# First and second score block of a head pair at one place, the third two steps behind, in a hybrid decoder layer

## The chip, the cores and the metric

The kernel runs on one core of one Trainium2 chip. The metric is the device time of one execution in microseconds; a version's time is the median of its runs. In the profile's rows PE is TensorE's matmuls, PEld its weight loads, DVE is VectorE, ACT is ScalarE, POOL is GpSimd, SP is SyncE, whose queue starts most DMAs.

## The reference

One decoder layer over a sequence of 1024 positions and 1024 channels, in float32. A normalised input goes through one large projection into eight groups of 1024 channels; two token mixers run beside each other and are merged by gates; an output projection and a squared-ReLU MLP follow. The change lies in the second mixer, a gated linear recurrence over 8 heads of 128 channels:

```python
def hybrid_mixer(h, lower_bound, w_in, ...):
    proj = h @ w_in
    xa, ga, q, f, v, g, m_a, m_b = jnp.split(proj, SPLIT_POINTS, axis=-1)
    y_a = rg_lru(causal_depthwise_conv(xa, conv_w, conv_b), ...) * gelu(ga)
    f_gate = lb + (1.0 - lb) * sigmoid(f)
    o = rms_norm(hgrn2_chunkwise(silu(q), (1.0 - lb) * sigmoid(-f), log(f_gate), v), hg_norm)
    y = sigmoid(m_a) * y_a + sigmoid(m_b) * (o * silu(g))
    return y @ w_out

# hgrn2_chunkwise, one chunk; cum is the cumulative sum of log f inside the chunk
o_inter = einsum('bhtk,bhkv->bhtv', qc * exp(cum), state)
decay = where(causal, exp(min(cum_t - cum_s, 0)), 0)
scores = einsum('bhtsk,bhsk->bhts', qc * decay, kc)
o_intra = einsum('bhts,bhsv->bhtv', scores, vc)
state = exp(last) * state + einsum('bhsk,bhsv->bhkv', kc * exp(min(last - cum, 0)), vc)
```

## The kernel before

The sequence is cut into two halves `c` of 512 positions and the heads into four pairs `p`, which makes eight head pairs `i = 4 * c + p`, 0 to 7. Matrix products in full precision are made of three matmuls each (`mm3`, lines 148 to 150: high by high, high by low, low by high parts), mostly with 128 weights' columns and 512 moving columns: the wide matmuls of the rows.

`stage(i)` is a generator that gives TensorE the projections of pair `i`: the values `v` of the pair before (16 steps, from the second pair on), then `xa` (8 steps), `q` (8 steps), five steps of `f`, the gates of the first mixer (`rg_lru`) and the rest of `f`. A step of a projection is two `mm3`, six wide matmuls. Other engines' work hangs between: ScalarE's copies of the convolution's input (`conv_in`), VectorE's convolution (`conv`, line 573), weight loads on SP's queue with their split into high and low parts (`fill_w`, line 92), and GpSimd's sums (`make_combos`). After the last pair, `last_stage` takes the place of a further stage; its first steps are `v` and the gate projection `g`.

`hgrn(c, p, got, go)` is the second mixer for one pair. It prepares decayed copies of queries and keys on VectorE (`q1`, `qa`, `qb` and `kk`, `kb`, `kc`, mostly by `mul`, line 668) and computes the scores inside groups of 2, 8 and 32 positions by three blocks of small matmuls (`blocks`, line 678): `pt1` from `kk` and `q1`, `pt2` from `kb` and `qa`, `pt8` from `kc` and `qb`. A block is 32 matmuls with 32 weights' columns and 48 moving columns, which the profile shows as 64 records; its results lie in one PSUM bank, for `pt1` and `pt2` one of the two with the tag `sc`. `own_block` (lines 668 and 689, tile `dd`) copies `pt1` under a mask on VectorE, `level_blocks` (line 697) does so for `pt2` and `pt8`. After `pt8` has read `kc` and `qb`, these are multiplied on in place, then `kk` and `qf` are made for the coarser blocks of lines 798 and 809; then come the transposes of `kk` (835), the state's products (845, added up on VectorE in lines 854 and 856) and the outputs (870, 873).

The interleaving is written out by hand: `go(n)` runs `n` steps of the next pair's stage, so the stage's matmuls fill the time between `hgrn`'s own. `GO`, `GO_FIRST` (pair 0) and `GO_SECOND_HALF` (pairs 4 to 7) hold the step counts; their first number is the step behind which `pt8` stands (26, in pair 0 it is 16, since stage 1 has no `v`), the second the steps from `pt8` to line 798. In the version before, `pt1` stands four steps and `pt2` two steps ahead of `pt8`.

TensorE's order in this part is the written one (`pin` keeps it in program order). The order on the other engines is set when the program is built, by a planner that takes the instruction of the smallest priority (the place in the program, or 400 places earlier under `tc.high_priority(400)`) among those that its own estimate of times finds ready. Engines run their queues in order and wait on semaphores.

## Time and profile before

| | |
|---|---|
| median of 3 runs | 1538.94 us (1538.2 to 1539.3) |
| the profiled execution: its time, its span | 1538.52 us, 1536.7 us |
| TensorE, busy share of the span | 99% |
| VectorE, ScalarE, GpSimd | 75%, 52%, 10% |
| granted TensorE clock | 0.998 |
| the first and the last score block of `pt1` begin at | 81.2 and 507.5 us |

A row of the timeline has the start, the duration, the engine, the line, the operation, the tile written and those read, the shapes and a count; in brackets stands the idle time of the engine ahead of it and what ended it. Matmuls overlap in their pipeline: a wide one is shown with 0.39 us, but the next one begins 0.23 us after it. A row of waits has the waiting engine with its tile and line, the one waited for, the sum in us, how often, and the longest. Rows of a line or a tile give the count and the least, median and largest duration in ns, and the first and last start.

### The profile page before, as it was taken

The numbers are of one execution on the slowest core, as the hardware profiler recorded it, in microseconds if no ns is written. First come the engines' busy times: TensorE is split into PE (matmuls) and PEld (weight loads), VectorE is DVE, ScalarE is ACT, GpSimd is POOL, SyncE is SP. The second block draws the span as 40 slices with busy tenths as digits, with TensorE's granted clock in tenths as the row PEclk, the third lists the DMA queues.
The fourth block names the chain that finished last, engine by engine and source line by source line (L and its number), as shares of the span: only waits on it lengthen the run. The fifth ranks groups of instructions, "written<-read, shape, count | busy, mean of one in ns | idle before, by whom it ended". The sixth has DMA issues, their size and how long they took to land. (4 is left out here: it accounts for less than half of the span.)

```text
span 1536.7 us, 23202 instructions
## 1 busy us (share of the span) xinstructions
PE 1522.4 (99%) x9085; PEld 1275.2 (83%) x9085; DVE 1149.0 (75%) x1656; ACT 804.6 (52%) x1341; POOL 153.6 (10%) x188
## 2 busy tenths in 40 slices
PE   9999999999999999999999999999999999999997
PEld 7878988889889888888888888888888788888886
DVE  6798695485675838786856578888888898888877
ACT  6646757567567335454533447666666721111115
POOL 1022210232624600000000000000000000000000
PEclk9999999999999999999999999999999999999999
DMA  8545455465674274432338324666666685666642
GB/s 298 200 153 193 150 193 200 147 217 174 224 232 140 99 298 165 151 137 83 137 106 329 127 110 161 261 251 249 249 253 247 229 308 223 249 252 251 250 182 110
DMA packets 81679, 306.82 MB, mean 200 GB/s; under 512 B 8481, under 2 KB 20897, under 8 KB 68642
## 3 DMA queue, kind: packets, MB, share of 16 engines
q1 hardware_dynamic: 77536, 292.75, 52.0%
q10 hardware_dynamic: 4034, 12.59, 2.1%
q8 instruction: 71, 1.16, 0.3%
q14 instruction: 38, 0.31, 0.1%
HBM read 201.50 MB, written 103.81 MB: 199 GB/s over the span
## 5 line engine op out<-in xcount | busy, mean ns | idle before, releaser
L1680 DVE TENSOR_TENSOR acc<-acc,dX 128x512 f32<-128x512 f32 x128 | 85.3, 686 | 28.2 <-PE dX L150 27.8
L87 ACT CAST wA<-q 128x512 fp32r<-128x512 f32 x46 | 28.5, 620 | 136.1 <-PE dX L150 101.6
L92 DVE TENSOR_TENSOR wL<-raw,wH 128x1024 fp32r<-128x1024 f32 x46 | 56.3, 1226 | 40.7 <-ACT wH L87 39.8
L87 ACT CAST wH<-raw 128x1024 fp32r<-128x1024 f32 x46 | 48.2, 1049 | 33.8 <-DMA raw<-wts_in 14.9
L1680 DVE TENSOR_TENSOR acc<-acc,dY 128x512 f32<-128x512 f32 x64 | 43.5, 687 | 13.3 <-PE dY L150 13.1
L148 PE MATMUL po<-wH,y 128*128 128x512 f32 x128 | 49.9, 393 | 0.0
L149 PE MATMUL po<-wL,y 128*128 128x512 f32 x128 | 49.9, 389 | 0.0
L150 PE MATMUL po<-wH,y 128*128 128x512 f32 x128 | 49.7, 390 | 0.0
L1531 ACT ACTIVATE b<-b 128x512 f32<-128x512 f32 x48 | 30.0, 625 | 29.2 <-DVE b L1530 29.0
L92 DVE TENSOR_TENSOR wA<-q,wA 128x512 fp32r<-128x512 f32 x46 | 31.5, 687 | 15.2 <-ACT wA L87 15.1
L112 ACT CAST wH<-raw 128x1024 fp32r<-128x1024 f32 x36 | 37.7, 1047 | 8.3 <-issue 3.7
L179 POOL TENSOR_TENSOR rstd_h<-rstd_h,mhalf 128x1 f32<-128x1 f32 x8 | 4.6, 583 | 370.8 <-DVE rstd_h L174 370.8
L573 DVE SCALAR_TENSOR_TENSOR xc<-xp,pvt,xc 128x512 f32<-128x512 f32 x48 | 40.2, 849 | 1.1 <-ACT xc L557 1.1
L1089 DVE TENSOR_TENSOR s<-q,q 128x512 f32<-128x512 f32 x46 | 31.7, 688 | 4.4 <-DMA q<-mlp_in 4.0
L486 POOL TENSOR_TENSOR stt<-r,stt 128x256 fp32r<-128x256 f32 x16 | 19.8, 1260 | 126.4 <-ACT stt L485 114.2
L1097 DVE TENSOR_TENSOR s<-q 128x512 f32<-128x512 f32 x46 | 31.6, 687 | 0.2
L1532 ACT ACTIVATE b<-b 128x512 f32<-128x512 f32 x48 | 30.1, 630 | 1.0
L877 ACT ACTIVATE on<-po 128x128 f32<-128x128 f32 x64 | 16.8, 277 | 26.1 <-PE po L873 26.0
L150 PEld LDWEIGHTS po<-wH,y 128*128 128x128 f32 x128 | 24.0, 188 | 5.0
L149 PEld LDWEIGHTS po<-wL,y 128*128 128x128 f32 x128 | 24.1, 188 | 4.8
L148 PEld LDWEIGHTS po<-wH,y 128*128 128x128 f32 x128 | 24.0, 188 | 4.8
L1179 DVE TENSOR_TENSOR gb<-gY,ge 128x512 f32<-128x512 f32 x14 | 9.7, 691 | 23.7 <-PE gY L150 23.7
(2562 smaller groups left out, 5439.1 us busy)
## 6 DMA issues: line engine op xcount, KB each, us to landing
q<-mlp_in SPq DMA_DIRECT2D x92, 512.0 KB, 3.7
raw<-wts_in SPq DMA_DIRECT2D x80, 512.0 KB, 5.0
rest<-wL SPq DMA_DIRECT2D x36, 512.0 KB, 2.9
wL<-rest SPq DMA_DIRECT2D x36, 512.0 KB, 4.3
hd<-ri SPq DMA_DIRECT2D x16, 256.0 KB, 3.5
od<-onT ACTq DMA_DIRECT2D x8, 512.0 KB, 6.6
cdT<-stT SPq DMA_DIRECT2D x16, 256.0 KB, 3.2
o<-od SPq DMA_DIRECT2D x4, 1024.0 KB, 7.2
```

The costliest lines, as they stand in the source:

```text
L87: ins = A.copy(h, src)
L92: ins = V.tensor_tensor(out=lo, in0=src, in1=h.bitcast(F32), op=ALU.subtract)
L112: A.copy(h, raw)
L148: pin(PE.matmul(o, ah, bh, start=first, stop=False, **how))
L149: pin(PE.matmul(o, ah, bl, start=False, stop=False, **how))
L150: pin(PE.matmul(o, al, bh, start=False, stop=last, **how))
L573: ins = V.scalar_tensor_tensor(xc[:, s, :], xp[:, j : j + T], pvt[:, PV_CW + 8 * j + u : PV_CW + 8 * j + u + 1], xc[:, s, :], op0=ALU.mult ...
L1089: ins = V.tensor_tensor(out=sa[:, 0, :], in0=a21, in1=a22, op=ALU.add)
L1097: V.tensor_tensor(out=sb[:, 0, :], in0=a21, in1=a11, op=ALU.add)
L1531: A.activation(b[:, at, :], b[:, at, :], AF.Relu, scale=-1.0 if at == 2 else 1.0)
L1532: A.activation(b[:, at, :], b[:, at, :], AF.Square)
L1680: V.tensor_tensor(out=dst, in0=dst, in1=banks[bk, pr], op=op)
```

## The change

`pt1` moves two steps back, directly ahead of `pt2`, so that both blocks stand together two steps ahead of `pt8`. Two pairs have places of their own: in pair 0 both stand three steps ahead of `pt8` (`pt1` one step later than before, `pt2` one earlier), in pair 6 both stand four steps ahead (`pt1` where it was, `pt2` two steps earlier). `pt8` and all that follows keep their steps. No instruction is added or removed.

```diff
+SCORES_AT = {0: (1, 0, 3), 6: (0, 0, 4)}
...
         at = GO_FIRST if first else GO_SECOND_HALF if c else GO
-        between = 2
-        go(at[0] - 2 * between)
+        before_1, before_2, before_8 = SCORES_AT.get(4 * c + p, (2, 0, 2))
+        go(at[0] - 4 + before_1)
         pt1 = blocks(kk, lambda k: q1[:, 16 * k : 16 * k + 16, :], "1")
-        go(between)
+        go(before_2)
         pt2 = blocks(kb, lambda k: qa[:, k * g0 // 32 : (k + 1) * g0 // 32, 1:7, :], str(c0))
-        go(between)
+        go(before_8)
         pt8 = blocks(kc, lambda k: q4[:, k * g1 // 32 : (k + 1) * g1 // 32, 1:7, :], str(c1), "hg")
...
-        go(at[1])
+        go(at[1] + 4 - before_1 - before_2 - before_8)
```

## The prediction

> **What bounds the kernel now.** I read the head of the page first, then TensorE's own waits in the stretch of the eight head pairs (70 to 540 us), then the order of its instructions around the score blocks.

> ```profile
> span 1536.7 us, 23202 instructions
> ...
> PE 1522.4 (99%) x9085; PEld 1275.2 (83%) x9085; DVE 1149.0 (75%) x1656; ACT 804.6 (52%) x1341; POOL 153.6 (10%) x188
> ```
> ```profile
> PE po L870 <- DVE sn L856: 0.9, 1, 0.9
> PE sc L809 <- DVE qf L668: 0.5, 1, 0.5
> PE pkv L845 <- ACT kT L840: 0.2, 1, 0.2
> ```

> The reader is to see that TensorE is the bound, and that in 470 us of mixer work only three waits of it are recorded, one of each kind. All three fall in pair 0 (their rows stand below, at 97.86, 104.39 and 110.15 us). Outside pair 0, then, anything that shortens TensorE's own stream shortens the kernel by the same amount, until some other engine comes too late. So the change is priced in TensorE's stream, and then I look for what becomes late. Pairs are numbered 0 to 7; A, B and C are the first, second and third score block (`sc<-q,kk`, `sc<-qa,kb` and `sc<-qb,kc` in the rows).

> **The price of one block.** These are rows of TensorE's timeline in pair 1 (start, duration, engine, line, operands, count), and the row of all A blocks in the answer for line 678:

> ```profile
> 137.70 0.39 PE L150 MATMUL pj_xa<-hT01H,wL 128*128 128x512 f32 x1
> 138.02 0.89 PE L678 MATMUL sc<-q,kk 128*32 128x48 f32 x64
> 138.84 0.50 PE L148 MATMUL pj_xa<-hT01H,wH 128*128 128x512 f32 x1
> 139.18 0.40 PE L149 MATMUL pj_xa<-hT01L,wH 128*128 128x512 f32 x1
> ...
> 139.64 0.40 PE L148 MATMUL pj_xa<-hT01H,wH 128*128 128x512 f32 x1
> 139.87 0.39 PE L149 MATMUL pj_xa<-hT01L,wH 128*128 128x512 f32 x1
> ...
> 141.46 0.39 PE L150 MATMUL pj_xa<-hT01H,wL 128*128 128x512 f32 x1
> 141.78 0.89 PE L678 MATMUL sc<-qa,kb 128*32 128x48 f32 x64
> ```
> ```profile
> L678 PE MATMUL sc<-q,kk x512: 205/206/231, 81.2 to 508.2; 128*32 128x48 f32 x171
> ```

> Twelve wide matmuls (two steps) lie between A and B. Their steady spacing is (141.46 - 139.64)/8 = 0.2275 us. From the wide matmul ahead of A (137.70) to the fifth one behind it (139.87) are 2.17 us; five wide spacings are 1.137 us; so A costs 1.035 us. The records of A themselves take less: the first starts at 138.02, the last at 138.02 + 0.89 - 0.21 (the median duration) = 138.70, that is 0.68 us for 64 records or 10.8 ns each. The remaining 0.355 us is the price of going from wide to narrow matmuls and back: 0.32 in place of 0.23 us ahead of the block, 0.14 us from its last record to the next wide one, and 0.34 in place of 0.23 us after that.

> **What the joining saves.** With B directly behind A, one way back and one way in are gone. If B's records go on at A's pace, B costs 0.68 in place of 1.035 us, and a pair saves 0.355 us. No row shows two blocks of this shape in a row. One bound is that inner pace; the other is the nearest joint of two narrow blocks, line 798 followed by line 809:

> ```profile
> 153.38 0.70 PE L798 MATMUL sc<-qb,kc 128*32 128x32 f32 x32
> 154.01 1.15 PE L809 MATMUL sc<-qf,kk 128*64 128x64 f32 x16
> ```

> Its last record starts about 0.20 us ahead of its end, at 153.88, so the joint took 0.13 us where one record inside A takes 0.011. By that, a pair saves 0.235 us. These two have different shapes (weights of 32 and of 64 columns), A and B have the same, so I take 0.355, the row that is nearest. [...]

> Pair 2 differs, because A stands behind transposes there:

> ```profile
> 134.32 1.03 PE L186 MATMUL xT_x<-ident,xn 128*128 128x128 f32 x8
> 135.11 0.48 PE L148 MATMUL pj_xa<-hT01H,wH 128*128 128x512 f32 x1
> ...
> 200.22 1.03 PE L186 MATMUL xT_x<-ident,xn 128*128 128x128 f32 x8
> 201.19 0.89 PE L678 MATMUL sc<-q,kk 128*32 128x48 f32 x64
> 202.00 0.50 PE L148 MATMUL pj_xa<-hT01H,wH 128*128 128x512 f32 x1
> ```

> From the transposes to the next wide matmul are 0.79 us without A and 1.78 us with it, so A costs 0.99 us plus the 0.02 us by which the second spacing differs: 1.01. Moved to B, the two cost 1.715 in place of 1.01 + 1.035, and pair 2 saves 0.33 us.

> **What the move makes late.** A's products are read on VectorE by the masked copy `dd<-sc,mf` (lines 668 and 689). Where A ends later, VectorE stops there, with everything queued behind: the copies of B and C (line 697), the convolution (573), and the products `kc`, `qb`, `kk`, `qf` that lines 798 and 809 wait for. The tightest of these are pairs 4 and 5, where the products take 1.23 us each. Rows of pair 4 on VectorE and TensorE, and VectorE's wait for score blocks in pairs 3 to 6:

> ```profile
> 325.94 0.42 DVE L668 TENSOR_TENSOR dd<-sc,mf 128x256 f32<-128x256 f32 x1
> ...
> 328.68 0.45 DVE L697 COPY_PREDICATED dd<-mu,sc 128x192 f32<-128x192 uint8 x1 [1.84 <-PE sc L678]
> ...
> 339.66 1.23 DVE L668 TENSOR_TENSOR qf<-qb,seg 128x512 f32<-128x512 f32 x1
> ```
> ```profile
> 327.72 0.89 PE L678 MATMUL sc<-qa,kb 128*32 128x48 f32 x64
> ...
> 342.67 1.15 PE L809 MATMUL sc<-qf,kk 128*64 128x64 f32 x16
> ```
> ```profile
> DVE dd L697 <- PE sc L678: 7.3, 4, 1.8
> ```

> Today VectorE copies A at once and then sits idle 1.84 us for B. Changed, A begins at 327.72 - 1.035 = 326.69 and is done 0.89 us later, at 327.58. VectorE then waits about 1.65 us ahead of A's copy, spends 0.9 us on it and comes to B at about 328.5, where B has been ready since 328.26. That is 0.2 us ahead of today's 328.68: one wait takes the place of the other. `qf` ends at 340.89 - 0.2, line 809 wants it at 342.67 - 0.355, and 1.6 us of slack are left. Pairs 3 and 5 go the same way. In pair 6 A keeps its place and B comes two steps earlier, so VectorE's idle time shrinks and nothing is late. The three others:

> ```profile
> 142.77 1.23 DVE L92 TENSOR_TENSOR wL<-raw,wH 128x1024 fp32r<-128x1024 f32 x1 [1.70 <-ACT wH L87]
> ...
> 206.39 0.43 DVE L668 TENSOR_TENSOR dd<-sc,mf 128x256 f32<-128x256 f32 x1
> ...
> 514.15 0.41 DVE L668 TENSOR_TENSOR dd<-sc,mf 128x256 f32<-128x256 f32 x1
> ```

> In pair 1 A is done at 141.78 - 1.035 + 0.89 = 141.64, and its copy fits into the 1.70 us in which VectorE waits for ScalarE until 142.77 anyway. In pairs 2 and 7 A's copy runs at 206.39 and 514.15, while the later A would be done at about 201.19 + 2.73 + 0.89 = 204.8 and 508.2 + 2.73 + 0.2 = 511.1 (2.73 us are the two steps): covered. What A is moved past otherwise: ScalarE's four copies of the convolution's input, in pair 7 one part of GpSimd's combinations, in pair 0 a weight load on SP's queue with its split; none of them waits for A. C keeps its step and comes 0.355 us earlier. I price all of this at nothing.

> **Pair 0.** Here TensorE already waits for others. Rows of TensorE, of VectorE, and the busy time of each engine in a window (PE, PEld, DVE, ACT, POOL):

> ```profile
> 96.21 0.39 PE L150 MATMUL pj_f<-hT01H,wL 128*128 128x512 f32 x1
> 96.65 0.70 PE L798 MATMUL sc<-qb,kc 128*32 128x32 f32 x32
> 97.86 1.12 PE L809 MATMUL sc<-qf,kk 128*64 128x64 f32 x16 [0.51 <-DVE qf L668]
> ...
> 104.39 2.05 PE L845 MATMUL pkv<-v,kT 128*128 128x128 f32 x16 [0.20 <-ACT kT L840]
> ...
> 110.15 0.57 PE L870 MATMUL po<-v,scT 128*128 128x128 f32 x3 [0.94 <-DVE sn L856]
> ```
> ```profile
> 97.01 0.70 DVE L668 TENSOR_TENSOR qf<-qb,seg 128x512 f32<-128x512 f32 x1
> ```
> ```profile
> 65.50:102.70 37.20, 36.64 (x389) 29.80 (x388) 37.08 (x67) 21.28 (x33) 5.51 (x6) 1.00 0.51 181
> ```

> VectorE is busy for 37.08 of 37.20 us: it does not wait for TensorE here, so a TensorE that is 0.355 us early at line 798 waits 0.355 us more, and the three waits behind it are set by the same queue. Pair 0 saves nothing as long as the order of VectorE's work stays. That order is the planner's, and the edit can shift it. Bounds: if all waits went, pair 0 would give 0.355 us and the waits themselves, 0.51 + 0.20 + 0.94 us plus up to 0.16 us each, because idle time counts from the modelled end of a matmul (0.39 against the spacing 0.23), and 0.12 us ahead of line 798 (0.44 against 0.32): about 2.6 us in all. If one weight split more (1.23 us, the row at 142.77) came ahead of `qf`, it would lose 1.23 us. I take 0, since nothing that VectorE finds ready in those 37 us changes by more than two steps.

> **Sum.** Pairs 1, 3, 4, 5, 6, 7: 6 x 0.355 = 2.13; pair 2: 0.33; pair 0: 0. Together -2.46 us. The profiled execution took 1538.52 us (span 1536.7 and 1.8 around it), so 1536.06; the median shown is 0.42 us above that execution, which gives 1536.5. With the dear joint it is 6 x 0.235 + 0.21 = 1.62 us, or 1537.3.

> **Rivals.** First, pair 0 gives too: VectorE's order there comes out better, TensorE's waits shrink, and the sum lies between -3.1 and -5.1 us, that is 1535.8 down to 1533.9; a middle is 1535.0. For it: B's products are ready a step earlier there. Against: the convolution (line 573) and ScalarE's `kT` stand behind the same total of VectorE work. Second, the planner puts one more VectorE operation ahead of a product that TensorE waits for: -2.46 + 1.23, 1537.7. For it: pair 0 has no slack; against: pairs 4 and 5 have 1.6 us.

> Third, the one on the other side: TensorE's sequencer cannot feed 128 narrow records in a row, and B runs at the pace at which it is fed. At line 798's pace (0.50 us for 31 spacings, 16 ns) B costs 1.03 us and the gain is gone: 1538.9. At line 809's (0.92 us for 15, 62 ns) it costs 3.95 us, 2.9 more than now, in seven pairs 20 us: 1559. It decides from 16 ns on, and the middle of the two paces gives 1549. Against it speaks this row:

> ```profile
> L678 PEldq EVENT_SEMAPHORE  x13: 51/51/51, 81.9 to 512.0; - x13
> ```

> The first of these semaphore waits for a score block is run at 81.9 us, right behind the first A and about 3 us ahead of the block that it serves: the sequencer is far ahead when a block ends. [...]

> **How the numbers follow.** Forecast 0.50 (own range 1536.1 to 1537.3), first rival 0.33, second 0.12, third 0.05. A measurement of this kernel tells about 0.2% (3.1 us) from no change. The first rival is faster by more than that (0.33), the forecast and the second lie within it (0.62), the third is slower (0.05). The range reaches from all of pair 0's waits gone, 1533.9, to the dear joint with one operation lost, -1.62 + 1.23, 1538.6, and leaves the third out.

> **What would show it.** Right: A and B as one run of 128 records with some 0.02 us between them, seven fewer entries of 0.32 us, VectorE idle ahead of `dd<-sc,mf` in pairs 3 to 5 in place of line 697, C 0.355 us earlier from pair to pair, and line 809 of pair 0 still at about 97.9 us. Wrong: a joint of 0.13 us or more, B longer than 0.9 us, a new TensorE wait on `qf`, `kc` or `pkv` outside pair 0, or pair 0's `po` earlier than 110 us.

## The result and the profile after

The changed kernel takes 1543.22 us (median of 12 runs, 1540.07 to 1547.43), the kernel before 1538.76 us beside it (12 runs, 1537.68 to 1539.62): ratio 1.0031, 95% interval 1.0023 to 1.0039. It is slower by 4.5 us where a gain of 2.5 us was forecast. The profiled execution of the changed kernel took 1541.38 us. The edit adds one line at the top, so every line number of its profile is one higher than before. From its page:

```profile
span 1539.6 us, 23205 instructions
...
PE 1520.7 (99%) x9085; PEld 1275.0 (83%) x9085; DVE 1145.8 (74%) x1656; ACT 805.4 (52%) x1341; POOL 151.2 (10%) x188
...
q8 instruction: 71, 1.16, 0.3%
```

The first two lines look as before; the span is 2.9 us longer although TensorE is busy for 1.7 us less. The third line is the one the prediction passed over: a DMA queue that carries instructions, 71 packets and 1.16 MB, so 16 KB each; the page of the kernel before has the same line. TensorE's records are 9085 matmuls, 9085 weight loads and 91 semaphore waits and drains of its sequencer; 18,261 / 71 is 257, so a packet holds about 256 of them. TensorE's waits (waiting engine, tile and line, the one waited for, sum in us, times, longest):

```profile
PE sc L679 <- issue: 2.9, 3, 2.0
...
PE pk L836 <- DVE kk L669: 0.4, 1, 0.4
...
PE gZ L151 <- DVE wA1235L L93: 0.2, 1, 0.2
```

The first row is new: three waits *inside* a score block, with nothing in the profile that released them ("issue"). Here they are on the timeline, in pairs 1, 3 and 5 (start, duration, engine, line, operands, count; idle time in brackets):

```profile
140.74 0.89 PE L679 MATMUL sc<-q,kk 128*32 128x48 f32 x64
141.44 0.86 PE L679 MATMUL sc<-qa,kb 128*32 128x48 f32 x64
142.24 0.50 PE L149 MATMUL pj_q<-hT00H,wH 128*128 128x512 f32 x1
...
145.18 0.62 PE L679 MATMUL sc<-qb,kc 128*32 128x48 f32 x37
147.76 0.53 PE L679 MATMUL sc<-qb,kc 128*32 128x48 f32 x27 [1.97 <-issue]
...
271.43 0.63 PE L679 MATMUL sc<-qb,kc 128*32 128x48 f32 x38
272.48 0.50 PE L679 MATMUL sc<-qb,kc 128*32 128x48 f32 x26 [0.43 <-issue]
...
394.37 0.87 PE L679 MATMUL sc<-qb,kc 128*32 128x48 f32 x58
395.72 0.29 PE L679 MATMUL sc<-qb,kc 128*32 128x48 f32 x6 [0.48 <-issue]
```

A and B behave as forecast: B starts 0.70 us after A, the next wide matmul 0.80 us after B, and no joint is seen. But C breaks after 37, 38 and 58 of its records. Before, it ran in one piece, here in pair 1:

```profile
145.54 0.89 PE L678 MATMUL sc<-qb,kc 128*32 128x48 f32 x64
```

Taken from the last record ahead of a gap, the three cost 2.18, 0.63 and 0.69 us. Counted from the start of the trace, 2242, 4545 and 6849 of TensorE's records stand ahead of them (matmuls, weight loads, and the sequencer's semaphore waits and drains): 2303 and 2304 apart, and 9 x 256 is 2304. So the three gaps stand at one place of a grid of 256 instructions, the size of a packet; such a place is called an edge below. What the other engines and the clock did there is in the rows by window, of the changed kernel and of the one before (PE, PEld, DVE, ACT, POOL busy, granted clock, DMA share, GB/s):

```profile
144.00:148.00 4.00, 2.03 (x63) 1.43 (x65) 3.42 (x8) 0.64 (x1) 0.00 (x0) 1.00 0.88 350
```
```profile
144.00:148.00 4.00, 4.00 (x79) 3.13 (x78) 4.00 (x8) 0.58 (x1) 0.15 (x1) 1.00 1.01 378
```

TensorE stands still for half of these 4 us, VectorE has less to do than before and not more, and the clock is full in both. The DMA packets between 145.3 and 146.3 us, just ahead of the end of the gap:

```profile
q1 hardware_dynamic: 105, 0.39, 97.7%
q8 instruction: 1, 0.02, 5.9%
```

One packet of instructions; 5.9% of 16 engines in 1.0 us is one transfer of 0.94 us. TensorE goes on 1.5 us after it has landed.

```
kernel, pair   asked    fetch begins (delay)   landed   next edge   window   gap
before  1     138.32       139.47 (1.15)       140.87    145.93      7.61     0
before  3     262.90       266.44 (3.53)       267.37    270.50      7.60     0
before  5     385.68       388.34 (2.66)       390.31    393.27      7.59     0
after   1     140.91       145.33 (4.42)       146.28    147.76      4.67    2.18
after   3     267.01       270.02 (3.00)       271.23    272.48      4.84    0.63
after   5     390.29       393.50 (3.20)       394.38    395.72      4.74    0.69
```

Before, the fetched piece had been there for 3 to 5 us when it was needed. After, the window is 2.8 to 2.9 us shorter and the gap ends 1.3 to 1.5 us after the landing. The delay of a fetch differs from one to the next, so the size of a gap does too. The span adds up: joints -2.46; the three gaps +3.50; smaller delays inside the same blocks and in A and B of pairs 3 and 4, +0.65; pair 7's `pk` +0.55; the weight parts at `gZ` and later +0.6; in all +2.84 of 2.9 us.

Rival II: the place of A does the harm, through VectorE, or any joined block does by itself. Rival III: a fixed price of a joined block in these pairs. The expectations of the first four runs use the numbers otherwise, and say how: there II is a limit on 256 narrow instructions in a row, wherever they stand, and III a new order of the other engines' work.

### The profile page after: what moved, and what is told of

It reads as the page before. It is cut to its first block, busy times and chain, and to the rows that moved or that the text cites. A ratio compares the mean times of both kernels' runs of the same rounds, so it can differ in the third digit from the quotient of the medians.

```text
span 1539.6 us, 23205 instructions
## 1 busy us (share of the span) xinstructions
PE 1520.7 (99%) x9085; PEld 1275.0 (83%) x9085; DVE 1145.8 (74%) x1656; ACT 805.4 (52%) x1341; POOL 151.2 (10%) x188
## 3 DMA queue, kind: packets, MB, share of 16 engines
q8 instruction: 71, 1.16, 0.3%
## 5 line engine op out<-in xcount | busy, mean ns | idle before, releaser
L1681 DVE TENSOR_TENSOR acc<-acc,dY 128x512 f32<-128x512 f32 x64 | 43.5, 686 | 13.3 <-PE dY L151 13.1
L149 PE MATMUL po<-wH,y 128*128 128x512 f32 x128 | 49.8, 393 | 0.0
L150 PE MATMUL po<-wL,y 128*128 128x512 f32 x128 | 49.8, 389 | 0.0
L150 PEld LDWEIGHTS po<-wL,y 128*128 128x128 f32 x128 | 24.1, 188 | 4.8
L149 PEld LDWEIGHTS po<-wH,y 128*128 128x128 f32 x128 | 24.0, 188 | 4.8
## 6 DMA issues: line engine op xcount, KB each, us to landing
q<-mlp_in SPq DMA_DIRECT2D x92, 512.0 KB, 3.7
raw<-wts_in SPq DMA_DIRECT2D x80, 512.0 KB, 4.8
rest<-wL SPq DMA_DIRECT2D x36, 512.0 KB, 2.9
wL<-rest SPq DMA_DIRECT2D x36, 512.0 KB, 4.0
od<-onT ACTq DMA_DIRECT2D x8, 512.0 KB, 6.8
```

Source lines behind the costliest of these rows:

```text
L149: pin(PE.matmul(o, ah, bh, start=first, stop=False, **how))
L150: pin(PE.matmul(o, ah, bl, start=False, stop=False, **how))
L1681: V.tensor_tensor(out=dst, in0=dst, in1=banks[bk, pr], op=op)
```

## The experiments

All kernels start from the changed one with its insertion put on an existing line, so that their profiles have the line numbers of before.

**Only the three pairs, and only the others.** The first run joins A and B in pairs 1, 3 and 5 alone, the second in all the others.

```diff
-SCORES_AT = {0: (1, 0, 3), 6: (0, 0, 4)}
+SCORES_AT = {0: (0, 2, 2), 2: (0, 2, 2), 4: (0, 2, 2), 6: (0, 2, 2), 7: (0, 2, 2)}
```

> Blocks stand together in pairs 1, 3 and 5 only; all other pairs as before. Theory I (TensorE's instructions arrive in pieces of 256, a piece is asked for only when the one before it is entered, and in pairs 1, 3 and 5 the 256 instructions behind that point run through in under 5 us, faster than a piece arrives): nearly all of the loss is here, about 1543 us, runs spread over several us, TensorE gaps of 0.5 to 2.5 us inside the third block of these pairs. Theory II (TensorE cannot be fed 256 narrow instructions in a row at their pace, wherever they stand): three of eight joints, a bit over a third of the loss, about 1540.5, gaps inside the joined blocks. Theory III (queues of the other engines in a new order): TensorE waits with a named engine ahead of lines 798, 809, 835 and no gap inside a block.

```diff
-SCORES_AT = {0: (1, 0, 3), 6: (0, 0, 4)}
+SCORES_AT = {0: (1, 0, 3), 6: (0, 0, 4), 1: (0, 2, 2), 3: (0, 2, 2), 5: (0, 2, 2)}
```

> Blocks stand together in pairs 0, 2, 4, 6 and 7 at the places of the change; pairs 1, 3 and 5 as before. Theory I: no gap over 0.5 us inside a block, a gain of 4 x 0.355 = 1.4 us less some 0.9 us of small losses in pairs 4 and 7, about 1538.3, runs as close together as those of before. Theory II: five of eight joints, about 1541.5. Theory III: as much of the loss as the waits of pair 7 make, 0.5 us.

The kernel before, beside them: 1538.41 us (27 runs). Pairs 1, 3 and 5 alone: 1546.62 us (5 runs, 1542.05 to 1547.65), ratio 1.0044 (1.0031 to 1.0057). The others alone: 1538.1 us (11 runs), 0.9995 (0.9986 to 1.0004). The waits of the first:

```profile
PE sc L678 <- issue: 3.5, 3, 1.3
```

The whole loss, and more, sits in these three pairs; the second run has no such row, and its C blocks are whole. So five joints alone break no C, against II, and the first run has no new wait that names another engine in the pairs, against III. The first run lies 3.6 us above its expected 1543 us; its profiled execution is the fastest (1542.05 us, mean granted clock 0.999), and three slower ones have 0.997. The second gains little: its joints should give 3 x 0.355 + 0.33 = 1.4 us, but B of pair 4 is drawn out by small gaps of 0.6 us in all, and pair 7 gives back some as well (below).

**The same order, other edges.** A block of 128 dummy instructions near the start moves every later edge by half a piece, in the changed kernel and in the kernel before.

```diff
-        fill_in(3)
+        fill_in(3); [keep(PE.matmul(idle[32 * b : 32 * b + 32, 48 * n : 48 * n + 48], ident[:, 32 * b : 32 * b + 32], ident[:, 0:48], start=True, stop=True)) for n in range(8) for b in range(4)]
```

> The changed kernel with one more block of 32 small matmuls (128 instructions, 64 of them weight loads) on TensorE near its start, into a bank that nobody reads, so every later instruction stands 128 places further in TensorE's stream; the order of work on all engines is otherwise the same. Theory I: the gaps leave pairs 1, 3 and 5 and come up in pairs 2, 4 and 7, where the limit of a piece now falls 84, 121 and 59 instructions into the joined blocks. Theories II and III: the gaps stay where they are. Time about 1544 in all cases, since the small matmuls cost some 1 us themselves.

> The kernel before with the same block of 32 small matmuls near the start, as the control of the run above. Theory I: no gap inside a block in any pair, since with two steps between all blocks 320 instructions always take at least 7.6 us; time of before plus 0.4 to 1.0 us, 1539.5. Theories II and III: the same.

Measured: 1540.78 us (11 runs), 1.0013 (1.0004 to 1.0022), and for the kernel before with the same block 1540.01 us (11 runs), 1.0008 (1.0000 to 1.0017). Waits and timeline of the first:

```profile
PE sc L678 <- issue: 2.5, 1, 2.5
```
```profile
146.00 0.89 PE L678 MATMUL sc<-qb,kc 128*32 128x48 f32 x64
...
209.03 1.12 PE L678 MATMUL sc<-qb,kc 128*32 128x48 f32 x64
...
331.44 0.71 PE L678 MATMUL sc<-qb,kc 128*32 128x48 f32 x47
334.69 0.38 PE L678 MATMUL sc<-qb,kc 128*32 128x48 f32 x17 [2.53 <-issue]
```

This is the plainest proof. TensorE's order in the pairs is the same, as is that of all 1656 instructions of VectorE and 1341 of ScalarE, and the gaps have left pairs 1, 3 and 5 (C in one piece) for pairs 4 (2.74 us) and 2 (0.18 us, seen in 1.12 instead of 0.89 us). They have 5825 and 3521 records ahead of them, 2241 + 14 x 256 and 2241 + 5 x 256: the grid of the changed kernel's gaps, to within one record. No price tied to a pair or to VectorE's work in it moves like that. The kernel before with the same block has no wait on "issue" in any score block. The windows of pairs 2, 4 and 7 are now 4.65, 4.76 and 5.40 us; the fetch of pair 7 was begun after 2.39 us and just made it, 2.04 us ahead of its use. The expected loss was too large by some 3 us, because in two of the three pairs the fetch came quickly. The dummy block itself costs 1.6 us, so with it the changed kernel stands only 0.8 us above the one before, and 2.4 us below itself without the block.

**A wider window.** A and B stay joined but stand earlier, five steps ahead of C: 60 instead of 24 wide instructions between B and C. The second run leaves pair 7 as before.

```diff
-SCORES_AT = {0: (1, 0, 3), 6: (0, 0, 4)}
+SCORES_AT = {0: (0, 2, 2), 2: (2, 0, 2)}
...
-SCORES_AT.get(4 * c + p, (2, 0, 2))
+SCORES_AT.get(4 * c + p, (-1, 0, 5))
```

> A and B joined in pairs 1 to 7, three steps earlier than in the changed kernel in pairs 1 and 3 to 7, and C where it was: 60 instead of 24 wide instructions stand between B and C (pair 2 stays as in the changed kernel, pair 0 as before). Theory I (TensorE's instructions come in pieces of 256, and two blocks close behind a joined pair leave too little time to fetch the next piece): in pairs 1, 3 and 5 the time from 64 instructions ahead of a piece to its end grows from about 4.8 us to 1.4 + 60 x 0.114 + 0.7 = 8.9 us, more than the 7.6 us that the kernel before had at its least. No gap inside a score block, 6 x 0.355 = 2.1 us less than before, at most 0.55 us given back in pair 7: 1536.3 to 1536.9 us. Rival II (the joined block itself loses in pairs 1, 3 and 5, through the later copies on VectorE or through any dense run of 256 instructions): gaps stay, 1541 to 1544 us.

```diff
-SCORES_AT = {0: (0, 2, 2), 2: (2, 0, 2)}
+SCORES_AT = {0: (0, 2, 2), 2: (2, 0, 2), 7: (0, 2, 2)}
```

> As the run with C five steps behind, but pair 7 with its three blocks two steps apart as before. Theory I: no gap inside a block, no wait of line 835 on VectorE's kk in pair 7 beyond the kernel before's; 5 x 0.355 + 0.33 - 0.355 (pair 2's share counted in) gives about 1.8 us less than before, 1536.6 us; in the trace the rows behind pair 7 stand 1.8 us ahead of the kernel before's, and those of the run with pair 7 joined 1.6 to 2.1. Rival II: 1541 to 1543 us.

The kernel before, beside them: 1538.47 us (21 runs). Measured: 1537.04 us (11 runs, 1536.5 to 1538.87), 0.9993 (0.9984 to 1.0001), and 1537.23 us (11 runs, 1536.95 to 1539.16), 0.9992 (0.9983 to 1.0001). Pair 1 of the first on the timeline:

```profile
136.88 0.89 PE L678 MATMUL sc<-q,kk 128*32 128x48 f32 x64
137.58 0.86 PE L678 MATMUL sc<-qa,kb 128*32 128x48 f32 x64
138.38 0.50 PE L148 MATMUL pj_xa<-hT01H,wH 128*128 128x512 f32 x1
...
145.40 0.89 PE L678 MATMUL sc<-qb,kc 128*32 128x48 f32 x64
```

No row of waits names "issue" on a score block in either run, and the windows of pairs 1, 3 and 5 are 8.53, 8.56 and 8.56 us, near the 8.9 that was expected. With these windows the joined blocks did no harm; rival II falls. About 6 us separate this kernel from the changed one; against the kernel before its median is lower by 1.4 us with an interval that includes 1, so a gain is not shown; it was the best tried. The median keeps 1.4 of the 2.5 us of its joints (six of 0.355 and pair 2's 0.33; the expectations of both runs count one joint too few). The profiled execution, at 1538.3 us, keeps only 0.2, and its waits show where most of the rest went:

```profile
PE pk L835 <- DVE kk L668: 1.6, 1, 1.6
```

This wait is in pair 1, at 160.9 us. VectorE there makes `kk` behind a normalisation product (line 180) for which it waits 2.03 us on GpSimd; in the kernel before `kk` stands ahead of that product, and there is no such wait. The run with pair 7 as before has it too, with 0.4 us. So behind pair 7 that run's rows stand 1.1 us ahead of the kernel before's, where 1.8 were expected, and those of the run with pair 7 joined stand level, where 1.6 to 2.1 were.

**A narrower window.** The changed kernel, but in pairs 1, 3 and 5 C stands directly behind B.

```diff
-SCORES_AT = {0: (1, 0, 3), 6: (0, 0, 4)}
+SCORES_AT = {0: (1, 0, 3), 6: (0, 0, 4), 1: (2, 0, 0), 3: (2, 0, 0), 5: (2, 0, 0)}
```

> The changed kernel, but in pairs 1, 3 and 5 C stands directly behind A and B, at their place: 384 narrow instructions in a row, A and B where the change put them. Theory I: the time from 64 instructions ahead of a piece to its end falls from 4.8 us to 320 x 0.0053 = 1.7 us. Where gaps arose, 5.4 to 6.9 us went from the one to the other; so each of the three pairs has a gap of some 4.4 us, 13 in all instead of the 3.5 us in the profile of the changed kernel, less 3 x 0.355 for the switches: about 1550 us (1546 to 1555). Rival II (the place of A and B, and what VectorE gets late from them, makes the loss): the loss stays as it is or falls by the switches, 1542 to 1543 us. Rival III (a fixed price of each joined block in these pairs): the same as II.

Measured: 1554.06 us (4 runs, 1551.66 to 1557.01), ratio 1.0101 (1.0087 to 1.0114), some 11 us above what rivals II and III expect. Pairs 1 and 5 on the timeline, and the granted clock (the third column from the end) in windows around the gap of pair 1 and behind those of pairs 3 and 5:

```profile
140.28 0.89 PE L678 MATMUL sc<-q,kk 128*32 128x48 f32 x64
140.99 0.86 PE L678 MATMUL sc<-qa,kb 128*32 128x48 f32 x64
141.67 0.72 PE L678 MATMUL sc<-qb,kc 128*32 128x48 f32 x49
148.54 0.55 PE L678 MATMUL sc<-qb,kc 128*32 128x48 f32 x15 [6.16 <-issue]
...
149.61 0.63 PE L149 MATMUL pj_q<-hT00L,wH 128*128 128x512 f32 x1
150.04 0.63 PE L150 MATMUL pj_q<-hT00H,wL 128*128 128x512 f32 x1
...
400.89 0.91 PE L678 MATMUL sc<-qb,kc 128*32 128x48 f32 x64
401.73 0.50 PE L148 MATMUL pj_q<-hT10H,wH 128*128 128x512 f32 x1
...
403.00 0.39 PE L150 MATMUL pj_q<-hT10H,wL 128*128 128x512 f32 x1
406.10 0.58 PE L148 MATMUL pj_q<-hT10H,wH 128*128 128x512 f32 x1 [2.71 <-issue]
```
```profile
142.00:148.50 6.50, 0.38 (x36) 0.24 (x23) 2.36 (x5) 1.43 (x3) 0.19 (x1) 0.80 1.00 355
148.50:150.00 1.50, 1.46 (x17) 1.19 (x18) 0.85 (x1) 0.80 (x2) 0.00 (x0) 0.50 0.25 87
150.00:154.00 4.00, 4.00 (x13) 3.17 (x12) 4.00 (x10) 1.24 (x2) 0.00 (x0) 0.65 0.00 0
...
278.00:282.00 4.00, 3.89 (x24) 3.05 (x24) 3.47 (x7) 1.24 (x2) 0.00 (x0) 0.63 0.04 14
...
406.00:410.00 4.00, 3.90 (x12) 3.11 (x12) 4.00 (x9) 1.34 (x5) 3.50 (x4) 0.65 0.32 109
```

Two things are to be read here. First, the gap keeps its place in the instruction stream. In the changed kernel pair 1 broke after 37 records of C; here the 12 wide matmuls between B and C have moved behind C, and it breaks after 37 + 12 = 49. Pair 5 broke after 58; here 58 + 12 = 70, which is all 64 of C and six wide matmuls, and there it stands, between two *wide* matmuls. It is no property of the narrow records. Second, the sum: the gaps are 6.37, 3.87 and 2.87 us, 13.1 where 13 was expected (by luck so close, as 4.4 was expected of each); but behind the first of them the clock falls to half (0.50 from 148.5 to 150 us), and wide matmuls come every 0.43 us instead of 0.23. Eight such matmuls behind 148.5 us cost 8 x 0.2 = 1.6 us, and the rows behind the other two gaps show much the same clock, 0.63 and 0.65. This is what the expectation lacked. How long a gap has to be for it the runs do not settle: here 6.37, 3.87 and 2.87 us brought the clock down, while behind the 2.74 us of the run with the dummy block it stood at 1.00 in every window from 328 to 345 us. In pair 5 the clock's share of 0.84 between 404 and 406 us puts its fall, if it went from 1.00 to 0.50 at once, some 2.4 us behind the start of the last matmul (403.00 us), as an estimate. The slowest runs of the changed kernel (1547.3 and 1547.4 us) have a mean granted clock of 0.996 and 0.997, the profiled one 0.999, so some of its spread of 7 us may be this; that is not shown, as no profile has the changed kernel with a gap that long.

## Why the prediction was wrong, step by step

**The price of a block and the joint: right.** A and B together cost 1.72 us on TensorE where 1.715 was reckoned, and 128 records stream in 1.36 us. In pair 1 of the changed kernel B begins 0.70 us after A, as one run. The dear bound, 0.13 us to a joint, was not needed. Where no gap disturbs it, a joined pair gains 0.32 to 0.36 us in the traces, so the 2.46 us of seven pairs were gained, or nearly so.

**Pair 0: right.** TensorE gets to line 798 earlier and waits for it there. Its rows in the changed kernel are these; the wait on `qf` is the 0.51 us of before, and that of line 798 has taken up most of the 0.355, so the waits of the first rival did not shrink:

```profile
97.01 0.70 PE L799 MATMUL sc<-qb,kc 128*32 128x32 f32 x32 [0.34 <-DVE qb L669]
98.21 1.12 PE L810 MATMUL sc<-qf,kk 128*64 128x64 f32 x16 [0.51 <-DVE qf L669]
```

**What the move makes late: here it failed.** The step went through VectorE, ScalarE, GpSimd and SP's queue, and priced "all of this at nothing". It left out one supply that TensorE has of its own, its instructions. The move changes their density: 320 instructions around an edge took 7.6 us and take 4.7. That costs 3.5 us at the edges and 0.65 us in smaller gaps in the profiled execution, more than the joints gain. The median execution loses 4.5 us where the profiled one loses 2.9; no profile shows what gaps it had.

**The third rival had the right engine and the wrong mechanism.** It asked whether the sequencer can feed 128 narrow records in a row. It can; the records of B run at A's pace. The limit lies in where 256 instructions end, and it strikes C. The semaphore row held against it (the wait for the next score block handled 3 us ahead) shows a lead in time, which among wide matmuls is long. Counted in instructions it is at least 24 (the records between that wait at 81.89 us and the block at 84.93), and inside a narrow block 24 of them pass in 0.13 us. The records of A and B go on at 10.8 ns. The instruction packets, 71 of 16 KB on the page of before, were not weighed. In the kernel before a fetch left no gap in pairs 1, 3 and 5, where each piece had landed 3 to 5 us ahead of its use; in the changed kernel, where 256 instructions ran in 1.4 us, the piece needed next landed 1.3 to 1.5 us ahead of the end of a gap.

**Pair 4: right; pairs 2 and 7: one right, one not.** In pair 4 VectorE waits 1.58 us ahead of A's copy, where 1.65 was reckoned, and no product is late:

```profile
329.67 0.42 DVE L669 TENSOR_TENSOR dd<-sc,mf 128x256 f32<-128x256 f32 x1 [1.58 <-PE sc L679]
```

In pair 2 TensorE has no new wait either. Pair 7 was called covered. VectorE there, after and before:

```profile
515.56 3.74 DVE L669 TENSOR_TENSOR seg<-seg 128x32 f32<-128x32 f32 x7
519.21 0.42 DVE L669 TENSOR_TENSOR dd<-sc,mf 128x256 f32<-128x256 f32 x1
519.55 1.27 DVE L1003 TENSOR_TENSOR g<-g,g 128x512 f32<-128x512 f32 x2
520.74 0.44 DVE L690 COPY_PREDICATED dd<-mu,sc 128x128 f32<-128x128 uint8 x1
```
```profile
513.42 0.81 DVE L668 TENSOR_TENSOR seg<-seg 128x32 f32<-128x32 f32 x2
...
514.48 1.13 DVE L668 TENSOR_TENSOR seg<-seg 128x32 f32<-128x32 f32 x2
515.53 0.43 DVE L689 COPY_PREDICATED dd<-mu,sc 128x128 f32<-128x128 uint8 x1
```

The planner has put A's copy behind all seven small products instead of two, and two products of the gate between its halves, so that the chain to `kk` ends later and `pk` waits. This is the second rival's mechanism, in another pair and for less: 0.55 us instead of 1.23. The run that joins all but pairs 1, 3 and 5 shows it too, and the run with pair 7 as before does not:

```profile
531.03 0.87 PE L835 MATMUL pk<-ident,kk 128*128 128x128 f32 x6 [0.41 <-DVE kk L668]
```
```profile
530.37 0.82 PE L835 MATMUL pk<-ident,kk 128*128 128x128 f32 x6
```

**What stays open.** Why a fetch begins sooner or later (1.15 to 9.18 us after "asked", in the traces of before and after) isn't settled. Other transfers explain a part at most: the median delay is 2.7 us in the 29 fetches where the mean busy share of the DMA engines during it was under a fifth, and 3.6 us in the 62 where it was over four fifths. The small gaps of 0.06 to 0.3 us inside A and B in pairs 3, 4 or 5, in several runs, do not lie on an edge; their cause wasn't found. Nor was it tried which order of VectorE would bring `kk` on time in pair 1 and yield the remaining gain.

## What to carry to other kernels

TensorE's instruction stream was a supply with a rate of its own here, 0.9 to 1.4 us for most transfers of 256: before small instructions are put together, count how many pass in the time of one fetch, and how far that lies from the edges of the pieces (here 256 instructions, and 5.4 to 6.9 us from asking to use at the three gaps of the changed kernel). If a new wait has no releaser, count the instructions ahead of it; if the counts differ by multiples of the piece's size, it points to the fetch, and a block of instructions put in earlier tests it: 128 of them near the start moved the gaps here. Room between dense blocks cured it here: the same joint with 60 wide instructions behind it had no gap, with 24 it had three.

## What the runs showed of the hardware

- In the three gaps of the changed kernel TensorE took a piece of 256 instructions into use 1.3 to 1.5 us after its landing. In the traces of before and after the transfer took 0.9 to 1.4 us in 136 of 142 fetches, and it began 1.15 to 9.18 us after the record 64 ahead of the piece before.
- The longest gap was paid twice: behind 6.4 us without instructions the granted clock stood at 0.50, and wide matmuls came every 0.43 instead of 0.23 us.
- The place of a fetch's edge moved with the number of instructions ahead of it: 128 more near the start of the kernel took the gaps from pairs 1, 3 and 5 to pairs 2 and 4.
